# A four-mixer block on one core: second buffers for two delta-rule inputs, other priorities and planned latencies, and side work on TensorE gathered into visits

## The chip, the cores and the metric

The kernel runs on one core of one Trainium2 chip. Times are device microseconds (us). The kernel before took 2264.02 us as the median of three runs (2262.28 to 2264.04). Five engines work side by side: TensorE (PE, with its weight loads as PEld), VectorE (DVE), ScalarE (ACT), GpSimd (POOL) and SyncE (SP), which only issues DMAs here.

## The reference

The input x has 512 tokens of 2048 channels. A normalized x is multiplied by one large matrix w_in, and the columns of the product feed four sequence mixers with 1024 channels each, and a gate z of 4096. The mixers' outputs, times silu(z), go through w_out and are added to x:

```python
h = rms_norm(x, norm_g[l])
p = jnp.einsum('bsd,dn->bsn', h, w_in[l])
p_rwkv, p_fox, p_gdn, p_diff, z = jnp.split(p, bounds, axis=-1)
y = jnp.concatenate([rwkv7_time_mix(p_rwkv, ...), forgetting_attention(p_fox, ...),
                     gated_deltanet(p_gdn, ...), differential_attention(p_diff, ...)], axis=-1)
x = x + jnp.einsum('bsm,md->bsd', y * jax.nn.silu(z), w_out[l])
```

Two mixers are recurrences over time. RWKV-7 updates a 64x64 state per head at each token. The gated delta rule (GDN) does the like with q, k and v that come out of a causal convolution of four taps and a silu; the reference states it by chunks, with a triangular solve in each chunk. The other two are softmax attentions with a decay (FOX) and as a difference of two maps (DIFF). All is float32.

## The kernel before, in words

**Products.** Float32 products with w_in and w_out are made of three float32r products each: hh·wh, hl·wh and hh·wl, with h and l for the rounded part and the rest. A weight tile `wr` of 512 KB comes by DMA on SP's queue (three buffers, L318); ACT rounds it to `wh` (L313) and DVE subtracts to `wl` (L314), two buffers each. `gemm_fm` makes 128 output channels for all 512 tokens (three matmuls of 512 columns, then a yield), `gemm_tm` makes 256 channels with tokens on partitions (matmuls of 256 columns, a yield after six).

**Passes.** `main` loops over j = 0..7; each j is 128 channels of each mixer. A pass streams, in this order, the products for RWKV r, k, v; GDN v, k, q; FOX q and k; both attentions' v; DIFF q and k. After the last pass the z products follow, first for 16 tiles of y with smaller j (two of them run in pass 0), then the other 16, and then the product with w_out.

**Threads.** Beside the stream, generators do the mixers' own work in small steps: `rwkv_local`, `gdn` (with `gdn_local`, then `inverses`), `rwkv_chain` (8 chunks of 64 tokens, three steps each), `gdn_chain` (4 chunks of 128), `fox` and `diff`. `inverses` solves 32x32 blocks on DVE (L970, L971: 31 steps) and merges them on PE; only then do both chains of that j start. The next j's RWKV blocks wait for the chain before (`until("rwkv_half", j-1, q)` in `rwkv_local`), the next `inverses` waits for those blocks (`until("BK", j)`), and `gdn_local` begins with `until("gdn_chain", j-1)`.

**The order on PE is written by a planner** at the end of `hybrid_kernel`, when the kernel is built. It keeps a clock `pe[0]`, to which every matmul adds its estimated cost (L65 to L75). A thread that yields `w` comes due at `pe + 1.25*w` (`spawn`, SLACK 1.25). While the stream is not held up, the planner takes a due thread ahead of the next step of the stream, so threads can be visited after any step of 0.64 us on that clock. `free(bank)` and `until(event)` poll in the same way, at 1.25 and 0.6 us. The stream yields what it needs before its products may leave PSUM, as `("gdn_chain", j-1)` before GDN's k and q leave it (their SBUF tiles `gc_k`, `gc_q` have one buffer each). While that is not done, the planner takes threads alone and sets the clock forward to each one's due time; no stream product then stands between their matmuls.

PE executes that order strictly, waiting on semaphores. The other engines' orders come from the tile framework's own simulated schedule, with priorities: `band(PRIO_CHAIN)` before `PRIO_W` (weight loads and splits), `PRIO_EVAC`, `PRIO_MIX` and last `PRIO_FILL`. `put_y` writes a mixer's finished y to DRAM; it is read again when z is gated.

Of the kernel before, what the change touches and what calls it, by code (L numbers as in the profile page):

```python
# [20 lines left out]
P = 128  # L21
# [21 lines left out]

SLACK = 1.25

PRIO_CHAIN = 0
PRIO_W = 1_000_000
PRIO_EVAC = 2_000_000
# [6 lines left out]
def hybrid_kernel(ctx: ExitStack, tc: tile.TileContext, ins, out, steps=tuple(range(NJ)), ydbg=None, tail=True):  # L55
# [3 lines left out]
    STT = nc.vector.scalar_tensor_tensor  # L59
    ACT = nc.scalar.activation  # L60
    pe = [0.0]

    def MM(o, a, b, side=1, **kw):

        n, m = math.prod(b.shape[1:]), math.prod(a.shape[1:])  # L65
        if a.dtype == F32:
            pe[0] += 4 * max(n, m, 32) / 2400 / side
        else:
            pe[0] += max(n, 256 if a.dtype == F32R else 128) / 2400 / side
        return nc.tensor.matmul(o, a, b, **kw)  # L70

    def transpose(o, a):
        pe[0] += 0.108
        return nc.tensor.transpose(o, a, ident)

# [140 lines left out]
    for part in range(4):  # L216
        if part == 2:
            load_x(1)
        wr = wp.tile([P, 1024], F32, name=f"w0r{part}", tag="wr", bufs=3) if part < 2 else \
            mp.tile([P, 1024], F32, name=f"w0r{part}")  # L220
        load_tm(wr, part, FOX0 + 2 * G, DIFF0 + 2 * G)
        w0.append((wr, mp.tile([P, 1024], F32R, name=f"w0h{part}"), mp.tile([P, 1024], F32R, name=f"w0l{part}")))
# [92 lines left out]
        return wh, wl  # L315

    def wtile():
        return wp.tile([P, WN], F32, name=f"wr{wcount[0]}", tag="wr", bufs=3)  # L318

    def gemm_fm(c0, name, then=None):  # L320
        acc = None
# [44 lines left out]
    ydr = [dr.tile([P, T], F32, name=f"ydr{m}") for m in range(MT)]  # L366

    def put_y(m, y):
        nc.sync.dma_start(ydr[m], y)
        if ydbg is not None:  # L370
            nc.sync.dma_start(ydbg[m], y)

# [321 lines left out]
    def rwkv_chain(j, st, XT):  # L694
# [7 lines left out]
        for c in range(NCH):  # L702
            AR, ET, BKt, ZV = (st[n][c // 4][:, c % 4] for n in ("AR", "ET", "BKt", "ZV"))
            yield from free("cr")
            ps = bank("cr", f"pC{j}_{c}", 1.0e9)

            for h in range(2):
                hs = slice(h * C, (h + 1) * C)
                MM(ps[0:R_, P + h * C:P + (h + 1) * C], ET[:, h, 0:R_], ZV[:, hs], start=True, stop=True)
            if c:  # L710
                MM(ps[:, 0:P], AR.rearrange("p a t -> p (a t)"), Sb, start=True, stop=True)
            nc.scalar.copy(rs[0:C], ps[0:C, P:2 * P])
            yield 2.4
            y = yt[(c % 2) * C:(c % 2 + 1) * C, c // 2, :]
            if c:
                band(PRIO_CHAIN)
                TT(rs[0:C], rs[0:C], ps[0:C, 0:P], op=ALU.add)
                band(PRIO_MIX)
                nc.scalar.copy(y, ps[C:P, 0:P])
            for h in range(2):  # L720
                hs = slice(h * C, (h + 1) * C)
                MM(ps[0:R_, 2 * P + h * C:2 * P + (h + 1) * C], ET[:, h, 0:R_], rs[:, hs], start=True, stop=True)
            yield 2.0
            band(PRIO_CHAIN)
            nc.vector.tensor_copy(ZV[0:C, :], ps[0:C, 2 * P:3 * P])
            band(PRIO_MIX)
            for h in range(2):
                hs = slice(h * C, (h + 1) * C)
                MM(ps[C:P, 3 * P + h * C:3 * P + (h + 1) * C], ET[:, h, R_:R_ + C], ZV[:, hs], start=True, stop=True)

            if c < NCH - 1:
                for h in range(2):
                    hs = slice(h * C, (h + 1) * C)
                    MM(ps[hs, P:P + C], BKt[:, h], ZV[:, hs], side=2, start=True, stop=True)
            pe[0] += 0.2
            if c < NCH - 1:
                band(PRIO_CHAIN)
                W = Wc[:, c:c + 1]
                tS = mp.tile([P, C], F32, name=f"tS{j}_{c}", tag="tS", bufs=1)
                for h in range(2):  # L740
                    hs = slice(h * C, (h + 1) * C)
                    if c:
                        TS(tS[hs, :], Sb[hs, hs], W[hs, :], None, op0=ALU.mult)
                for h in range(2):
                    hs = slice(h * C, (h + 1) * C)
                    o = ps[hs, P:P + C]
                    if c:
                        STT(Sb[hs, hs], o, W[hs, :], tS[hs, :], op0=ALU.mult, op1=ALU.add)
                    else:
                        TS(Sb[hs, hs], o, W[hs, :], None, op0=ALU.mult)  # L750
                band(PRIO_MIX)
            if c:
                TT(y, y, ps[C:P, 3 * P:4 * P], op=ALU.add)
            else:
                nc.scalar.copy(y, ps[C:P, 3 * P:4 * P])
            release(f"pC{j}_{c}", 3.0)
            if c % 4 == 3:
                done.add(("rwkv_half", j, c // 4))

# [24 lines left out]
    def gdn_evac(j, i, acc):  # L784
        s = "qkv"[i]
        n = 8 * i + j
        if s == "v":
            a = mp.tile([P, T], F32, name=f"gc_{s}{j}", tag="gc_v", bufs=1)
        else:
            a = mp.tile([P, T], F32, name=f"gc_{s}{j}", tag=f"gc_{s}", bufs=1)  # L790
        ACT(a, acc, AF.Copy, scale=convw(3, n))
        for d in (1, 2, 3):
            STT(a[:, d:T], acc[:, 0:T - d], convw(3 - d, n), a[:, d:T], op0=ALU.mult, op1=ALU.add)
        return a
# [19 lines left out]
        return pt  # L814

    def gdn_local(j, res):

        yield from until("gdn_chain", j - 1)
        GA = mp.tile([P, NT, 2, P], F32, name=f"GA{j}", tag="GA", bufs=1)
        Dm = GA[:, :, 1, :]  # L820
        nc.gpsimd.dma_start(Dm, gcd[:, j, :].unsqueeze(0).to_broadcast([P, NT, P]))
        gdn_silu(j, "v", res["v"])
        yield 2.5
        band(PRIO_FILL)
        for c in range(NT):
            for b in range(4):
# [5 lines left out]
                                fill=0.0, base=0, channel_multiplier=-1)  # L832
        band(PRIO_MIX)

        yield from until("gk", j)
        k2 = res["k"]
        gdn_silu(j, "k", k2)
        yield 7.0
        yield from free("tr")
        pt = gdn_transposed(j, "k", k2)  # L840
        KTs = mp.tile([P, NT, P], F32, name=f"KTs{j}", tag="KTs", bufs=1)
# [15 lines left out]
        vn = mp.tile([P, NT, P], F32, name=f"vn{j}", tag="vn", bufs=1)  # L857
        TT(vn, pt.rearrange("p (t f) -> p t f", f=P), vn_s.unsqueeze(2).to_broadcast([P, NT, P]), op=ALU.mult)

        yield from until("gq", j)  # L860
        q2 = res["q"]
        gdn_silu(j, "q", q2)
        yield 8.0
        for q in range(2):
            yield from free("sc")
            ps = psc(f"pK{j}_{q}", 2.5)
# [16 lines left out]
    def gdn_chain(j, st, XG):  # L883
# [3 lines left out]
        for c in range(NT):  # L887
# [3 lines left out]
            if c:  # L891
                MM(ps[:, 0:P], k2[:, cs], S, start=True, stop=True)
                MM(ps[:, P:2 * P], q2[:, cs], S, start=True, stop=True)
                rs = mp.tile([P, P], F32, name=f"grs{j}_{c}", tag="gs", bufs=4)
                band(PRIO_CHAIN)
                STT(rs, ps[:, 0:P], eg_neg[:, c, j:j + 1], vn[:, c, :], op0=ALU.mult, op1=ALU.add)
                band(PRIO_MIX)
                ACT(ot[:, c, :], ps[:, P:2 * P], AF.Copy, scale=eg[:, 0, c, j:j + 1])
            else:
                rs = vn[:, 0, :]  # L900
            yield 2.4
            MM(ps[:, 2 * P:3 * P], XG[:, c, :], rs, start=True, stop=True)
            Y = mp.tile([P, P], F32, name=f"gY{j}_{c}", tag="gs", bufs=4)
            band(PRIO_CHAIN)
            nc.scalar.copy(Y, ps[:, 2 * P:3 * P])
            band(PRIO_MIX)
            yield 2.4
            if c < NT - 1:
                MM(ps[:, 0:P], KTs[:, c, :], Y, start=True, stop=True)
            MM(ps[:, 3 * P:4 * P], GA[:, c, 1, :], Y, start=True, stop=True)  # L910
# [8 lines left out]
            else:  # L919
                TS(ot[:, c, :], ps[:, 3 * P:4 * P], -1.0, None, op0=ALU.mult)  # L920
            band(PRIO_MIX)
            release(f"pG{j}_{c}", 3.2)
        done.add(("gdn_chain", j))
        sq = mp.tile([P, T], F32, name=f"osq{j}", tag="tmp", bufs=2)
        ACT(sq, ot.rearrange("p t f -> p (t f)"), AF.Square)
# [23 lines left out]
    def inverses(j, ET, GA, blk, start_rwkv):  # L949
# [14 lines left out]
        nc.gpsimd.memset(Xf[64:112, 1:512:34], 1.0)  # L964
        pr = lcp.tile([112, 512], F32, name=f"bP{j}", tag="lc", bufs=8)
        for t in range(1, 32):
            band(PRIO_FILL)
            n, w = (t + 1) // 2, t + 1
            pv_ = pr[:, 0:n * w].rearrange("p (a b) -> p a b", b=w)
            TT(pv_, X[:, 0:n, 0:w], A[:, 0:w, t].unsqueeze(1).to_broadcast([112, n, w]), op=ALU.mult)  # L970
# [20 lines left out]
        XQ = mp.tile([P, 4, 32], F32, name=f"XQ{j}", tag="gs", bufs=4)  # L991
        for g in range(4):
            nc.gpsimd.dma_start(XQ[32 * g:32 * g + 32], xb[16 + g:32:4].rearrange("m s t -> s m t"))
        yield 14.5
        yield from until("rwkv_local", j)

        XN = lcp.tile([P, 16, 32], F32, name=f"XN{j}", tag="lc", bufs=8)
# [84 lines left out]
    def qk_heads(j, ev, kind):  # L1082
# [1 line left out]
        gi = 0 if kind == "fox" else 2  # L1084
        TS(ss, ss, 1.0 / C, 1e-6, op0=ALU.mult, op1=ALU.add)
        rs = rsqrt(mp, ss, 16, "qk", f"{kind}{j}")
        yield 3.0
        rv = rs.rearrange("p (t s h) -> p t s h", t=NT, s=2)
        for s, dst in enumerate((qa, ka)):
            dv = dst.rearrange("p t (h f) -> p t h f", f=C)  # L1090
            TT(dv, dv, rv[:, :, s].unsqueeze(3).to_broadcast([P, NT, 2, C]), op=ALU.mult)
        yield 1.2

        parts = []
        for s, src in enumerate((qa, ka)):
# [189 lines left out]
    def main():  # L1285
# [15 lines left out]
        for j in steps:  # L1301
# [21 lines left out]
            for i in (2, 1, 0):  # L1323
                s_ = "qkv"[i]
                acc = yield from gemm_fm(GDN0 + i * G + j * P, f"g{s_}{j}")
                yield "gdn_chain" if i < 2 else "gdn_local", j - 1
                band(PRIO_EVAC)
                gres[s_] = gdn_evac(j, i, acc)
                done.add(("g" + s_, j))
                if i == 2:  # L1330
                    spawn(2.5, gdn(j, gres, local))
# [36 lines left out]
        v_evac(V0)(b, accs0[b])  # L1368

    stream, need = main(), None  # L1370
    with tc.manual_schedule(engines={nc.tensor.engine}):
        while stream is not None or threads:
            wait = stream is None or (need is not None and need not in done)
            if threads and (wait or threads[0][0] <= pe[0]):
                at_, _, gen = heapq.heappop(threads)
                pe[0] = max(pe[0], at_)
                band(PRIO_MIX)
                try:
                    spawn(next(gen), gen)
                except StopIteration:  # L1380
                    pass
            else:
                try:
                    need = next(stream)
                except StopIteration:
# [108 lines left out]
```

## Time and profile before

| | |
|---|---|
| median of 3 runs | 2264.02 us |
| the profiled execution | 2263.21 us, of which its span 2261.5 us |
| granted TensorE clock, mean over the span | 0.993 |
| busy: PE, PEld, DVE, ACT, POOL | 2209.2, 1893.5, 1363.8, 804.5, 246.7 us |
| chain that ended last, by engine | PE 90%, DVE 5%, POOL 2%, DMA 1%, ACT 1%, issue 1% |
| DMA | 226.33 MB, mean 100 GB/s |

Matmuls are pipelined: a row's duration (0.39 us for 512 columns) is longer than the distance to the next start, and the distances of starts tell the rate. "Idle before" is the engine's own wait ahead of an instruction, and behind the arrow stands what ended it. A pass is the time from one j's first `acc_r` product to the next j's.

### The profile page before, as it was taken

To read this page: it belongs to the slowest core of one execution; us is meant where nothing else is said; L and a number is where in the kernel's file an instruction comes from. 1 tells how busy PE (TensorE), PEld (TensorE's weight loads), DVE (VectorE), ACT (ScalarE), POOL (GpSimd) and SP (SyncE) were. 2 spreads that over 40 slices of the span, in tenths; PEclk is the share of its full clock that TensorE was granted. 3 is DMA by queue.
4 is the path that set the end of the run, shared out by engine and by line. 5 is a ranking of instruction groups with operands and counts; after the bars stand their busy time and mean duration, and the time that the engine had idled before them with its cause. 6 is when DMAs were issued, how large, how long until landed. Compare 5 with 4: busy or idle time off the path is not lost.

```text
span 2261.5 us, 37256 instructions
## 1 busy us (share of the span) xinstructions
PE 2209.2 (98%) x14604; PEld 1893.5 (84%) x14604; DVE 1363.8 (60%) x3601; ACT 804.5 (36%) x1504; POOL 246.7 (11%) x506
## 2 busy tenths in 40 slices
PE   7999999999999999999999999899999999999999
PEld 6789789879878977987997897798788888888887
DVE  6368588576857957767685695776553434322222
ACT  4233443443353343344335334334422223321121
POOL 2200121112102011110210211111000000100000
PEclk9999999999999999999999999999999999999999
DMA  5433323323322332332332333233346444654443
GB/s 167 104 88 94 97 74 90 97 66 94 98 72 73 93 96 58 94 101 61 85 107 63 80 82 98 65 96 105 96 137 181 119 125 120 163 136 116 113 125 75
DMA packets 321874, 226.33 MB, mean 100 GB/s; under 512 B 17423, under 2 KB 285394, under 8 KB 321186
## 3 DMA queue, kind: packets, MB, share of 16 engines
q1 hardware_dynamic: 298722, 187.05, 31.3%
q0 software_dynamic: 9152, 15.37, 3.2%
q10 hardware_dynamic: 13824, 21.54, 2.9%
q8 instruction: 115, 1.88, 0.3%
q14 instruction: 61, 0.50, 0.1%
HBM read 203.93 MB, written 19.97 MB: 99 GB/s over the span
## 4 chain that ended last, share of the span: by engine, by line
PE 90%; DVE 5%; POOL 2%; DMA 1%; ACT 1%; issue 1%; SPq 0%; ACTq 0%; DVEq 0%
PE acc_z L70 16%; PE acc_o L70 15%; PE acc_dqk L70 8%; PE acc_fqk L70 8%; PE acc_vv L70 6%; PE acc_k L70 4%; PE acc_v L70 4%; PE acc_r L70 4%; PE acc_gv L70 4%; PE acc_gk L70 4%; PE pC L70 3%; POOL GA L828 2%; PE acc_gq L70 2%; PE pG L70 1%; PE pSf L70 1%; DMA GA<-gcd 1%
## 5 line engine op out<-in xcount | busy, mean ns | idle before, releaser
L314 DVE TENSOR_TENSOR wl<-wr,wh 128x1024 fp32r<-128x1024 f32 x318 | 389.0, 1224 | 534.5 <-ACT wh L313 527.7
L313 ACT CAST wh<-wr 128x1024 fp32r<-128x1024 f32 x318 | 333.9, 1050 | 750.8 <-PE acc_o L70 231.8
L70 PE MATMUL acc_z<-hh,wh 128*128 128x512 f32 x512 | 204.5, 399 | 0.0
L70 PE MATMUL acc_z<-hh,wl 128*128 128x512 f32 x512 | 199.7, 390 | 0.0
L70 PE MATMUL acc_z<-hl,wh 128*128 128x512 f32 x512 | 199.6, 390 | 0.0
L70 PE MATMUL acc_o<-wh,gl 128*128 128x512 f32 x512 | 183.6, 389 | 0.0
L70 PE MATMUL acc_o<-wl,gh 128*128 128x512 f32 x512 | 177.6, 389 | 0.0
L70 PE MATMUL acc_o<-wh,gh 128*128 128x512 f32 x512 | 176.2, 389 | 0.0
L70 PE MATMUL acc_fqk<-wh,hh 128*128 128x256 f32 x512 | 151.8, 296 | 0.8 <-DVE gssk L807 0.8
L70 PE MATMUL acc_fqk<-wl,hh 128*128 128x256 f32 x512 | 145.1, 283 | 0.0
L70 PE MATMUL acc_fqk<-wh,hl 128*128 128x256 f32 x512 | 144.9, 283 | 0.0
L70 PE MATMUL acc_dqk<-wh,hh 128*128 128x256 f32 x512 | 138.2, 292 | 0.0
L970 DVE TENSOR_TENSOR bP<-bX,bA 112x2 f32<-112x2 f32 (+30 forms) x248 | 122.1, 492 | 24.1 <-POOL bA L958 18.5
L70 PE MATMUL acc_dqk<-wh,hl 128*128 128x256 f32 x512 | 133.6, 283 | 0.0
L70 PE MATMUL acc_vv<-wh,hh 128*128 128x256 f32 x448 | 120.4, 290 | 0.0
L70 PE MATMUL acc_vv<-wh,hl 128*128 128x256 f32 x448 | 116.9, 282 | 0.0
L70 PEld LDWEIGHTS acc_z<-hh,wl 128*128 128x128 f32 x512 | 96.1, 188 | 20.5
L70 PEld LDWEIGHTS acc_o<-wl,gh 128*128 128x128 f32 x512 | 96.1, 188 | 20.2 <-DVE wl L314 0.3
L70 PEld LDWEIGHTS acc_o<-wh,gl 128*128 128x128 f32 x512 | 96.1, 188 | 20.0
L70 PEld LDWEIGHTS acc_o<-wh,gh 128*128 128x128 f32 x512 | 96.0, 188 | 20.1 <-ACT wh L313 0.2
L70 PEld LDWEIGHTS acc_z<-hh,wh 128*128 128x128 f32 x512 | 96.2, 188 | 19.4 <-issue 0.7
L70 PEld LDWEIGHTS acc_z<-hl,wh 128*128 128x128 f32 x512 | 96.3, 188 | 18.4
(515 smaller groups left out, 5226.4 us busy)
## 6 DMA issues: line engine op xcount, KB each, us to landing
wr<-in_w_in SPq DMA_DIRECT2D x162, 512.0 KB
wr<-in_w_in SPq DMA_DIRECT2D x184, 256.0 KB
wr<-in_w_out SPq DMA_DIRECT2D x64, 512.0 KB
zy<-ydr ACTq DMA_DIRECT2D x30, 256.0 KB
nb<-cdr SPq DMA_DIRECT2D x8, 512.0 KB
xo<-in_x ACTq DMA_DIRECT2D x16, 256.0 KB
gr<-gdr POOLq DMA_DIRECT2D x16, 256.0 KB, 5.1
out<-xo ACTq DMA_DIRECT2D x16, 256.0 KB
```

The source lines that it names most:

```text
L70: return nc.tensor.matmul(o, a, b, **kw)
L313: nc.scalar.copy(wh[:, 0:n], wr[:, 0:n])
L314: TT(wl[:, 0:n], wr[:, 0:n], wh[:, 0:n].bitcast(F32), op=ALU.subtract)
L828: nc.gpsimd.tensor_scalar(Dm[:, c, bs], Dm[:, c, bs], gcx[:, b, c * 8 + j:c * 8 + j + 1], 0.0, op0=ALU.subtract, op1=ALU.min)
L970: TT(pv_, X[:, 0:n, 0:w], A[:, 0:w, t].unsqueeze(1).to_broadcast([112, n, w]), op=ALU.mult)
```

## The change: what it does

1. **Buffers.** `gc_k` and `gc_q` get two buffers, `wr` two in place of three. The stream's k and q now need only the chain of j-2. `gdn_local` does all three silus first, each as soon as its product is there, and only then waits for the chain of j-1.
2. **Bands and queues.** The copy of y in the RWKV chain (L719) and the scaling of `ot` in the GDN chain (L898) move from MIX to CHAIN. The solve's 31 steps move from FILL to MIX. `put_y` issues on POOL's queue in place of SP's.
3. **Planned latencies.** Shorter in both chains and ahead of the merge of the inverses, longer in `qk_heads`.
4. **Visits.** A thread may be taken only when the stream has run at least STRETCH = 1.5 us of the planner's clock since its last return from threads that issued matmuls, or while such a visit lasts (`away`), or when the stream is held up.

```diff
-        wr = wp.tile([P, 1024], F32, name=f"w0r{part}", tag="wr", bufs=3) if part < 2 else \
+        wr = wp.tile([P, 1024], F32, name=f"w0r{part}", tag="wr", bufs=2) if part < 2 else \
...
-        return wp.tile([P, WN], F32, name=f"wr{wcount[0]}", tag="wr", bufs=3)
+        return wp.tile([P, WN], F32, name=f"wr{wcount[0]}", tag="wr", bufs=2)
...
-        nc.sync.dma_start(ydr[m], y)
+        nc.gpsimd.dma_start(ydr[m], y)
...
-            yield 2.4
+            yield 1.8
             y = yt[(c % 2) * C:(c % 2 + 1) * C, c // 2, :]
             if c:
                 band(PRIO_CHAIN)
                 TT(rs[0:C], rs[0:C], ps[0:C, 0:P], op=ALU.add)
+                nc.scalar.copy(y, ps[C:P, 0:P])
                 band(PRIO_MIX)
-                nc.scalar.copy(y, ps[C:P, 0:P])
...
-            yield 2.0
+            yield 1.5
...
-            release(f"pC{j}_{c}", 3.0)
+            release(f"pC{j}_{c}", 2.4)
...
-            a = mp.tile([P, T], F32, name=f"gc_{s}{j}", tag=f"gc_{s}", bufs=1)
+            a = mp.tile([P, T], F32, name=f"gc_{s}{j}", tag=f"gc_{s}", bufs=2)
...
     def gdn_local(j, res):
+        gdn_silu(j, "v", res["v"])
+        yield 2.5
+        yield from until("gk", j)
+        k2 = res["k"]
+        gdn_silu(j, "k", k2)
+        yield 2.5
+        yield from until("gq", j)
+        q2 = res["q"]
+        gdn_silu(j, "q", q2)
+        yield 2.5
 
         yield from until("gdn_chain", j - 1)
...
-        gdn_silu(j, "v", res["v"])
-        yield 2.5
...
-        yield from until("gk", j)
-        k2 = res["k"]
-        gdn_silu(j, "k", k2)
-        yield 7.0
...
-        yield from until("gq", j)
-        q2 = res["q"]
-        gdn_silu(j, "q", q2)
-        yield 8.0
+        yield 4.0
...
+                ACT(ot[:, c, :], ps[:, P:2 * P], AF.Copy, scale=eg[:, 0, c, j:j + 1])
                 band(PRIO_MIX)
-                ACT(ot[:, c, :], ps[:, P:2 * P], AF.Copy, scale=eg[:, 0, c, j:j + 1])
...
-            yield 2.4
+            yield 2.0
             MM(ps[:, 2 * P:3 * P], XG[:, c, :], rs, start=True, stop=True)
...
-            yield 2.4
+            yield 1.8
...
-            release(f"pG{j}_{c}", 3.2)
+            release(f"pG{j}_{c}", 2.6)
...
-            band(PRIO_FILL)
+            band(PRIO_MIX)
             n, w = (t + 1) // 2, t + 1
...
-        yield 14.5
+        yield 12.5
         yield from until("rwkv_local", j)
...
-        yield 3.0
+        yield 4.0
         rv = rs.rearrange("p (t s h) -> p t s h", t=NT, s=2)
...
-        yield 1.2
+        yield 2.0
...
-                yield "gdn_chain" if i < 2 else "gdn_local", j - 1
+                yield ("gdn_chain", max(j - 2, steps[0] - 1)) if i < 2 else ("gdn_local", j - 1)
...
+    away, since = False, 0.0
...
-            if threads and (wait or threads[0][0] <= pe[0]):
+            ready = threads and threads[0][0] <= pe[0] and (away or pe[0] - since >= STRETCH)
+            if threads and (wait or ready):
                 at_, _, gen = heapq.heappop(threads)
                 pe[0] = max(pe[0], at_)
                 band(PRIO_MIX)
+                n = issued[0]
                 try:
                     spawn(next(gen), gen)
                 except StopIteration:
                     pass
+                away = away or issued[0] > n
             else:
+                if away:
+                    away, since = False, pe[0]
```

`issued` counts the calls of MM and transpose.

## Rows read from the trace of the kernel before

**Rows 1.** The page: engines' busy us (share of the span), and costly groups.

```profile
PE 2209.2 (98%) x14604; PEld 1893.5 (84%) x14604; DVE 1363.8 (60%) x3601; ACT 804.5 (36%) x1504; POOL 246.7 (11%) x506
...
L970 DVE TENSOR_TENSOR bP<-bX,bA 112x2 f32<-112x2 f32 (+30 forms) x248 | 122.1, 492 | 24.1 <-POOL bA L958 18.5
```

**Rows 2.** Waits of PE: instruction <- what ended it, us in total, times, longest us.

```profile
PE pC L70 <- ACT yt L719: 20.0, 7, 3.4
...
PE ptfox L74 <- DVE qafox L1091: 6.1, 6, 1.1
```

**Rows 3.** Passes 2, 3 and 4 by engine; behind the busy times PEclk, DMA, GB/s.

```profile
413.00:598.00 185.00, 181.18 (x1402) 158.91 (x1401) 133.47 (x402) 74.21 (x156) 26.45 (x55) 1.00 0.31 82
598.00:788.00 190.00, 185.48 (x1417) 161.90 (x1416) 135.81 (x404) 76.38 (x160) 27.79 (x57) 0.98 0.32 84
788.00:978.00 190.00, 184.55 (x1418) 161.37 (x1417) 135.63 (x405) 76.30 (x160) 26.79 (x57) 0.99 0.32 84
```

**Rows 4.** Timeline of PE, 680 to 693 us: start, duration, instruction, count, wait.

```profile
680.48 1.16 PE L70 MATMUL pA<-AR,BK 64*128 64x128 f32 x16
681.57 0.45 PE L70 MATMUL pC<-ZV,ET 128*66 128x64 f32 x4
...
686.39 0.71 PE L70 MATMUL pC<-rs,ET 128*66 128x64 f32 x4 [3.44 <-ACT yt L719]
...
687.30 0.77 PE L70 MATMUL acc_gq<-hh,wh 128*128 128x512 f32 x1
...
692.62 0.27 PE L70 MATMUL pC<-ZV,ET 128*64 128x64 f32 x1
```

**Rows 5.** Busy times by engine just after that wait.

```profile
688.00:692.00 4.00, 4.00 (x11) 3.13 (x10) 3.70 (x22) 1.78 (x3) 0.72 (x1) 0.50 0.52 60
```

**Rows 6.** Timeline of PE: the first and the last short run between two visits.

```profile
244.06 0.60 PE L74 MATMUL pPf<-ident,prf 128*128 128x128 f32 x4
...
245.99 0.45 PE L70 MATMUL pmr<-XN,ET 32*32 32x32 f32 x32
...
1661.71 0.39 PE L70 MATMUL acc_z<-hh,wl 128*128 128x512 f32 x1
1661.94 0.60 PE L74 MATMUL pgo<-ident,vn 128*128 128x128 f32 x4
1662.29 0.48 PE L70 MATMUL acc_z<-hh,wh 128*128 128x512 f32 x1
1662.61 0.40 PE L70 MATMUL acc_z<-hl,wh 128*128 128x512 f32 x1
...
1663.86 0.27 PE L70 MATMUL pC<-ZV,ET 128*64 128x64 f32 x1
```

**Rows 7.** Timeline of PE: one turn from RWKV chain to RWKV chain.

```profile
631.46 0.40 PE L70 MATMUL pC<-ZV,ET 128*66 128x64 f32 x4
...
731.37 0.45 PE L70 MATMUL pC<-ZV,ET 128*64 128x64 f32 x4
...
740.71 0.60 PE L74 MATMUL pB<-ident,BK 128*128 128x128 f32 x4
...
814.73 0.45 PE L70 MATMUL pmr<-XN,ET 32*32 32x32 f32 x32
...
821.62 0.40 PE L70 MATMUL pC<-ZV,ET 128*66 128x64 f32 x4
```

**Rows 8.** Timelines of DVE and PE: a chain step's sum, and the matmul on it.

```profile
658.96 0.27 DVE L717 TENSOR_TENSOR rs<-rs,pC 64x128 f32<-64x128 f32 x1
...
661.68 0.40 PE L70 MATMUL pC<-rs,ET 128*66 128x64 f32 x4
```

**Rows 9.** Weight splits while z streams (DVE, ACT), and a DMA of the page.

```profile
1702.90 1.23 DVE L314 TENSOR_TENSOR wl<-wr,wh 128x1024 fp32r<-128x1024 f32 x1 [4.06 <-ACT wh L313]
...
1712.74 1.05 ACT L313 CAST wh<-wr 128x1024 fp32r<-128x1024 f32 x1 [4.38 <-PE acc_z L70]
...
gr<-gdr POOLq DMA_DIRECT2D x16, 256.0 KB, 5.1
```

More of the change, by code (lines that the diff above doesn't have):

```diff
@@ L44 @@
 SLACK = 1.25
+STRETCH = 1.5
 PRIO_CHAIN = 0
@@ L61, in hybrid_kernel @@
     pe = [0.0]
+    issued = [0]
     def MM(o, a, b, side=1, **kw):
+        issued[0] += 1
         n, m = math.prod(b.shape[1:]), math.prod(a.shape[1:])
@@ L72, in transpose @@
     def transpose(o, a):
+        issued[0] += 1
         pe[0] += 0.108
```

## The prediction

> **What bounds the kernel now.** I read the page first, then PE's waits, the passes, and PE's order row by row. The page gives TensorE 98% of the span and POOL 11% [rows 1]: no other engine is near, so time can only go where PE waits, runs at the lower clock, or spends more than its products need. Each has its view.
>
> *Waits.* One place holds most of the wait: seven times a matmul of the RWKV chain waits, 20.0 us in all, and six times the FOX transposes, 6.1 us [rows 2]. The timeline shows where the first kind sits [rows 4]: between GDN's k and q products. There the stream needs `("gdn_chain", j-1)`, so the planner lines up thread work alone: pA, pC, pB, then the pC that waits 3.44 us. Nothing streams in between, so PE reaches a chain step before ACT and DVE have done theirs.
>
> *Clock.* Right behind that wait the granted clock is 0.50 (1.2 GHz) for the whole of 688 to 692 us, against 1.00 (2.4 GHz) in an undisturbed pass [rows 3, 5]. Twelve q products take 5.32 us there [rows 4]; at the 0.23 us from one start to the next that full clock shows [rows 6], they take 2.76.
>
> *Passes.* Pass 2 (413 to 598) takes 185 us at 1.00; pass 3 takes 190 at 0.98, pass 4 190 at 0.99, and three more like it follow [rows 3]. The difference is that wait and its clock.
>
> *Changes between stream and threads.* Take the visit of four transposes at 1661.94 [rows 6]. From the last z product's start before it to the second one's after it is 0.90 us. Two stream steps take 0.46, four transposes at the pace of sixteen pA (1.09/16 = 0.068 us each, [rows 4]) 0.27. The visit itself costs 0.17; half of it is the first product after it, 0.32 to the next start in place of 0.23. From 230 us on there are 461 visits, some 58 a pass, and 174 of them follow a run of only one or two steps of the stream (first and last in [rows 6]).
>
> **The change part by part**, against the profiled execution (2263.2 us: span 2261.5 and 1.7 around it; the median shown, 2264.0, is 0.8 above).
>
> 1. *Second buffers of k and q; need of j-2.* The hold between k and q is gone. The same thread matmuls must still run, now with stream products between them, so only waits and clock are gained: -20.0 us; clock 2.6 in pass 3 and up to 1% of 190 = 1.9 us in each of four passes, together -10. Upper end -30; lower end 0, if the same step is late elsewhere. I take -30, and charge new lateness in 5.
>
> 2. *qk_heads 3.0 to 4.0 and 1.2 to 2.0.* The last of these waits, about 1 us each [rows 2], is met by 0.8 x 1.25 = 1.0 us more lead, and the first yield gives another 1.25. -6 (0 to -6.1).
>
> 3. *Visits.* On the planner's clock a step is 0.64 us, so 1.5 us means three steps: the 174 visits after shorter runs move to the next allowed point and mostly join another. Each joined visit saves at most 0.17; a change from thread to thread may cost something of its own, though sixteen pA pass into pC without a gap [rows 4]. I take 0.13: 174 x 0.13 = -22.6. Bounds: 0 if visits only shift, and 231 x 0.17 = -39 if half of the 461 go.
> The Trainium skill ("TensorE: Matmul & The Clock Gate", Part 2, step 1) says that PE pulls the next weight load ahead of running matmuls, so the next tile's weights load meanwhile; by that rule a return would cost nothing and this part would give 0, 2238 in all. The 0.32 against 0.23 us speaks against it.
>
> 4. *What threads lose by waiting for a visit.* The loop that could set the pace is RWKV's [rows 7]: chain from 631.46 to 731.37 (99.9 us), blocks to 740.71 (9.3), solve to 814.73 (74.0), merge to the next chain's start at 821.62 (6.9): 190 us, as long as the pass. Eight chunks lose (0.6 + 0.5 + 0.6) x 1.25 = 2.1 us each, 17 in all; the merge is due 2.5 us sooner. The stretch rule adds to some 40 resumptions in that loop (24 of the chain, 7 of the solve, the rest polls and blocks) between 0 and 1.3 us each; with 2 in 5 visits held back I take 0.35: +14. The loop comes out near 190 - 19.5 + 14 = 184, less some 3 us because visits get cheaper: 181. PE's own work in a pass is 190 - 3.4 - 1.05 - 1.9 - 58 x 0.38 x 0.13 (2.9) = 181. Both meet; neither adds.
>
> 5. *Shorter chain latencies.* PE waits in order, so a late sum stops the stream behind it. In the crowded stretch rs is ready at 659.23 and its matmul starts at 661.68 [rows 8]: 2.45 us of lead, of which the change takes 0.75. So most steps stay covered. Priority of L719 and L898 helps a little. I charge 1.3 us a pass, +10 in all; ends: 0, and 0.4 us on each of 288 chain steps, +115 (a rival).
>
> 6. *The solve from FILL to MIX.* 122.1 us of products over 248 instructions [rows 1], and their sums, no longer give way to softmax work emitted later. 0; up to +20 if FOX's transposes wait for it, down to -5 where the merge had waited.
>
> 7. *Two `wr` buffers.* A third tile in flight goes; the load of tile n+2 now starts when tile n is split. In the z stretch this is 1704.13, and the cast of n+2 starts at 1712.74, 8.6 us later, waiting for PE, not for DMA [rows 9]. A 256 KB transfer lands 5.1 us after its issue there; doubling all of that would be 10, and behind the cast a tile's 24 products give PE 24 x 0.23 = 5.5 us, of which cast and subtraction take 1.05 + 1.23. So 0; +10 at most, in the columns of w_out where x and the output move too.
>
> 8. *put_y on POOL, silus first, GA later.* 32 issues leave SP, where a late y held back weights behind it, and stand in POOL's order instead; y is not read before z is gated. POOL is 11% busy [rows 1]. 0, -3 to +5. GA's DMA and POOL work now starts with the wait for the chain, beside the k transposes; `inverses` waits for the RWKV blocks anyway, 0.
>
> Sum: -30 - 6 - 22.6 + 10 = -48.6; 2263.2 - 48.6 = 2214.6, and with the 0.8 of the median **2215 us**. By passes: five from about 190 to 182 (-40), two from 185 to 182 (-5), 3 in the stretch of z with threads: the same.
>
> **The rivals.**
> - *The thread loop sets the pace.* If held visits cost 0.5 us a resumption more than I took, the loop is 187 to 189, the stream runs ahead until it needs `rwkv_local` or, at the end, `inverses`. It gains about 2 us in five passes and 3 behind: 2250 (2236 to 2262). For it: the loop equals the pass today [rows 7]. Against: the hold slows the loop itself, 3.44 us of wait in one chunk.
> - *Chain steps come late.* This ends on the other side. DVE, 71% busy in a pass (135.81 of 190, [rows 3]), executes in a fixed order; with 0.6 to 0.75 us less lead, and solve steps ahead of softmax, PE meets unfinished sums. 288 chain steps: the gain of 59 us is gone at 0.2 us a step; at 0.35 it is +100, **2305**, the lower clock behind longer waits included. For it: the 3.44 us are of this kind. Against: 2.45 us of lead in a full stretch.
> - *Changes cost nothing, or visits do not get fewer*: 2215 + 22.6 = 2238.
> - *Half the visits go, and nothing new waits*: 2263 - 30 - 6 - 39 = 2188, 2189 as a median.
>
> **How the numbers follow.** Chances: forecast 0.48 (own range 2200 to 2232), loop 0.20, late chain 0.17, no gain from visits 0.06, half the visits 0.09. About 0.2% (4.5 us) is what a measurement can tell from no change. Slower: 0.16 out of the late chain. Within: 0.01 of it and 0.04 of the loop's top. Faster: the rest, 0.79. For the range I leave out the late chain's 0.16 at the top and 0.04 below 2180: 2180 to 2264.
>
> **What would show it.** Right: no wait of pC on L719 near 3.4 us and clock 1.00 in all passes; ptfox waits gone; some 290 visits from the second pass on in place of 461; no stream run under three steps except beside a hold; passes of 181 to 183 us. The loop rival shows as passes of 187 or more, or as threads alone on PE ahead of RWKV's r or of the z tiles; the late chain as many waits of pC, pG or pPf on DVE and ACT. It is wrong if PE waits for `wl` or `wh`, or if there are fewer visits and the time per visit grows as much.

## The result, and the profile after

| | before | after |
|---|---|---|
| median of the runs of this comparison | 2263.15 us (2261.82 to 2264.04) | **2236.96 us** (2235.21 to 2238.55) |
| span of the profiled execution | 2261.5 us | 2233.4 us |
| mean granted TensorE clock | 0.993 | 0.997 |

The ratio is 0.9885, with a 95% interval of 0.9867 to 0.9902: 26 us faster, where 49 were forecast. The time lies inside the range, but outside the forecast's own 2200 to 2232.

The page after, busy time of the engines, and the solve's line that [rows 1] showed (busy, mean ns | idle before it):

```profile
span 2233.4 us, 37352 instructions
...
PE 2197.7 (98%) x14604; PEld 1890.0 (85%) x14604; DVE 1377.5 (62%) x3601; ACT 799.5 (36%) x1504; POOL 260.1 (12%) x538
...
L977 DVE TENSOR_TENSOR bP<-bX,bA 112x2 f32<-112x2 f32 (+30 forms) x248 | 122.1, 492 | 9.4 <-POOL bA L965 4.4
```

The same number of matmuls keeps PE busy for 11.5 us less. PE's waits after (us in total, times, longest), to be read against [rows 2]:

```profile
PE pC L75 <- ACT yt L724: 12.1, 14, 2.5
...
PE pC L75 <- DVE ZV L731: 1.7, 3, 0.6
...
PE acc_o L75 <- ACT wh L319: 0.7, 1, 0.7
```

The 3.4 us waits and all six of ptfox are gone. But the profile still shows the RWKV chain waiting on the copy of y, 14 times and shorter: 12.1 us where there were 20.0. Passes 2, 3 and 4 after, in the columns of [rows 3]:

```profile
413.00:599.00 186.00, 184.06 (x1434) 161.39 (x1432) 137.70 (x404) 77.39 (x161) 28.79 (x61) 1.00 0.32 88
599.00:782.00 183.00, 181.07 (x1407) 159.78 (x1404) 137.22 (x403) 74.36 (x159) 29.17 (x61) 1.00 0.32 86
782.00:968.00 186.00, 184.04 (x1433) 161.23 (x1432) 138.70 (x405) 77.45 (x163) 28.81 (x61) 1.00 0.32 86
```

The clock is 1.00 in these passes, and in those behind them; pass 1 has one fall of it, behind a wait of 2.5 us (323 to 327 us: 0.57). From pass 2 on they take 182 to 186 us, on average 184.3 (before 189.2) and not 181 to 183. So the waits and the clock came back about as forecast, and the rest has to be looked for inside PE's busy time. From the starts of all PE rows between the start of pass 2 (413 us) and the first z product (six passes) I split the time into five parts. The stream alone, 806.3 us, is the same in every kernel. "Border" is what PE needs above that rate when it enters a visit and at the first product after it; "inside" is from the first start of a visit to the first start of the stream behind it, less the waits, and the change of thread is part of it:

| us in six passes | before | after | after, no stretch rule | before, stretch rule only | before, buffers only | last two runs: rule and short latencies / neither |
|---|---|---|---|---|---|---|
| PE waits | 30.3 | 11.4 | 13.3 | 33.6 | 7.7 | 17.7 / 4.4 |
| lower clock and rest | 11.3 | 4.1 | 4.9 | 10.1 | 4.3 | 5.5 / 4.4 |
| border | 45.8 | 36.1 | 43.7 | 37.2 | 43.3 | 36.7 / 43.8 |
| inside visits | 241.1 | 247.5 | 238.8 | 255.0 | 237.5 | 245.1 / 236.8 |
| visits | 352 | 300 | 360 | 282 | 370 | 300 / 365 |
| sum with the stream | 1135 | 1106 | 1107 | 1142 | 1099 | 1111 / 1096 |

From before to after: waits -18.9, clock and rest -7.2, border -9.7, inside +6.4; together -29.4. What is new is in the row "inside visits": two thirds of what the border saves come back there.

One gathered visit after the change, PE's timeline (start, duration, instruction, count):

```profile
663.00 0.39 PE L75 MATMUL acc_gk<-hh,wl 128*128 128x512 f32 x1
663.23 0.95 PE L75 MATMUL pn<-bonesr,rw_k 128*128 128x2 f32 x8
664.04 0.47 PE L75 MATMUL pd<-V,prd 128*128 128x128 f32 x2
664.44 0.44 PE L75 MATMUL pSd<-Khdiff,Qhdiff 64*128 64x384 f32 x2
...
665.16 0.45 PE L75 MATMUL pC<-ZV,ET 128*66 128x64 f32 x4
665.45 0.44 PE L75 MATMUL pC<-Sb,AR 128*128 128x128 f32 x2
665.72 0.39 PE L75 MATMUL pG<-Sg,gc_k 128*128 128x128 f32 x2
665.95 0.39 PE L75 MATMUL pG<-Sg,gc_q 128*128 128x128 f32 x2
666.09 0.48 PE L75 MATMUL acc_gk<-hh,wh 128*128 128x512 f32 x1
666.41 0.39 PE L75 MATMUL acc_gk<-hl,wh 128*128 128x512 f32 x1
```

Four threads share one way back, at the old price: 0.32 us from 666.09 to the next start. Before the stream, the two gc_q products take 0.14 us (665.95 to 666.09). In the kernel before, the same two stand ahead of another thread's products and take 0.33 (timeline of PE, before):

```profile
678.73 0.49 PE L70 MATMUL pG<-Sg,gc_k 128*128 128x128 f32 x2
679.06 0.39 PE L70 MATMUL pG<-Sg,gc_q 128*128 128x128 f32 x2
679.39 1.16 PE L70 MATMUL pd<-V,prd 128*128 128x128 f32 x8
```

So it is with three of four kinds of group in the kernel before (median from first start to the next start behind the group): pG's four matmuls 0.36 us between stream and stream (5 cases) and 0.66 between threads (7), six pSd 0.55 (8) and 0.91 (6), six pC 0.43 (27) and 0.56 (13). Eight pC are free of it, 0.49 in both places.

### The profile page after: what moved, and what is told of

It reads as the page before. It is cut to its first block, busy times and chain, and to the rows that moved or that the text cites. A ratio compares the mean times of both kernels' runs of the same rounds, so it can differ in the third digit from the quotient of the medians.

```text
span 2233.4 us, 37352 instructions
## 1 busy us (share of the span) xinstructions
PE 2197.7 (98%) x14604; PEld 1890.0 (85%) x14604; DVE 1377.5 (62%) x3601; ACT 799.5 (36%) x1504; POOL 260.1 (12%) x538
## 4 chain that ended last, share of the span: by engine, by line
PE 90%; DVE 3%; DMA 3%; POOL 3%; ACT 2%; issue 1%; SPq 0%; ACTq 0%; DVEq 0%; POOLq 0%
PE acc_z L75 16%; PE acc_o L75 15%; PE acc_dqk L75 8%; PE acc_vv L75 8%; PE acc_fqk L75 7%; PE acc_v L75 4%; PE acc_k L75 4%; PE acc_r L75 4%; PE acc_gv L75 3%; PE acc_gk L75 3%; PE pC L75 3%; POOL GA L842 2%; PE acc_gq L75 2%; DMA GA<-gcd 2%; PE pG L75 1%; PE pSf L75 1%
```

## The experiments

The medians of before beside these runs are 2262.91 to 2263.49 us; each ratio is to the runs of before on the same chip.

**The stretch rule taken out** of the changed kernel.

```diff
-STRETCH = 1.5
+STRETCH = 0.0
```

> The changed kernel with STRETCH = 0.0: threads are taken as soon as they are due, as before the change; all else as changed. The order on PE then has 496 visits in place of 420. Theory A (joined visits save little, about 0.08 us each, since a change from thread to thread costs nearly as much as one from and to the stream): about +6 us, 2243 (2240 to 2247), waits of the chains as they were or a few us more. Theory B (a visit costs the 0.17 us that I read off one of them): +13 us, 2250 or more. Theory C (gathering costs more in late chain steps than it saves): faster than 2237.

Measured: 2238.0 us, ratio 0.9893 (0.9878 to 0.9908): 1 us from the changed kernel, which the intervals can't tell from nothing, and none of the three theories. The table's columns two and three show why: 60 visits fewer save 7.6 us at the border and cost 8.7 inside.

**The stretch rule alone**, put into the kernel before (its lines of the change and `issued`, nothing else).

```diff
+STRETCH = 1.5
...
+            ready = threads and threads[0][0] <= pe[0] and (away or pe[0] - since >= STRETCH)
+            if threads and (wait or ready):
```

> The kernel before with the stretch rule alone: 399 visits in place of 490, one buffer for k and q, old bands, old latencies, three weight buffers. Theory A (0.08 us a visit): -7 us, about 2256, the waits of 3.4 us between k and q still there. Theory B (0.17 us): -15 us, about 2248. Theory C (held visits lengthen the chain loop, which then sets the pace): longer holds ahead of q, 2263 or slower.

Measured: 2277.69 us, ratio 1.0067 (1.0054 to 1.0079): slower, as in theory C. Waits of PE and passes 3 to 5, in the columns of [rows 2, 3]:

```profile
PE pC L74 <- ACT yt L724: 18.6, 14, 3.6
```

```profile
605.00:797.00 192.00, 185.47 (x1419) 162.81 (x1418) 137.01 (x405) 76.35 (x161) 27.43 (x57) 0.98 0.30 80
797.00:988.00 191.00, 186.02 (x1414) 162.35 (x1413) 139.48 (x405) 75.44 (x158) 27.05 (x57) 0.98 0.32 85
988.00:1176.00 188.00, 182.91 (x1420) 160.76 (x1419) 134.38 (x402) 76.10 (x160) 27.38 (x57) 1.00 0.31 83
```

By the table the border is 8.6 us less than before, but PE's waits are 3.3 more and the inside 13.9. The passes fit a loop of the recurrences that is longer because every resumption waits for a visit, with the holds still in the stream; how much of the 13.9 is threads that run alone, and how much changes between threads, this run doesn't part.

**The buffers alone**: part 1 of the change in the kernel before.

```diff
-            a = mp.tile([P, T], F32, name=f"gc_{s}{j}", tag=f"gc_{s}", bufs=1)
+            a = mp.tile([P, T], F32, name=f"gc_{s}{j}", tag=f"gc_{s}", bufs=2)
...
-                yield "gdn_chain" if i < 2 else "gdn_local", j - 1
+                yield ("gdn_chain", max(j - 2, steps[0] - 1)) if i < 2 else ("gdn_local", j - 1)
```

(with the silus ahead of the wait and two `wr`)

> The kernel before with the second buffers of gc_k and gc_q, two weight buffers, the need of j-2 and the three silus first in gdn_local; nothing else of the change. Theory A (the removed hold is nearly all of the gain): the waits of 3.4 us and the half clock behind them go, passes of 184 to 185 us, 2240 (2235 to 2247); the FOX transposes still wait 1 us a pass. Rival (the hold only moves, because the chain loop of 190 us sets the pace): passes stay at 188 to 190, about 2258.

Measured: 2239.75 us, ratio 0.9898 (0.9884 to 0.9911). This is 23.5 of the 26 us. The copy of y, 20.0 us before, is down to this (PE's waits):

```profile
PE pC L70 <- ACT yt L719: 0.6, 2, 0.4
```

Its six passes are even 6 us shorter than those of the changed kernel. It gives that back at the end: from the first z product on it takes 722 us, the changed kernel 715. There PE waits 4.1 us in place of 0.7, and the clock is at 0.50 for 6.8 us from 1562 us on. The last pass's threads reach 160 us into z in place of 143, but that this is the reason isn't shown: in the run with short latencies in the last pass, below, they reach 140, and the stretch still takes 719.

**The latencies of before** in the changed kernel: 2.4, 2.0 and 3.0 in the RWKV chain, 2.4, 2.4 and 3.2 in GDN's, 14.5 before the merge.

```diff
-            yield 1.8
+            yield 2.4
             y = yt[(c % 2) * C:(c % 2 + 1) * C, c // 2, :]
...
-        yield 12.5
+        yield 14.5
```

> The changed kernel with the planned latencies of before in both chains and ahead of the merge (2.4, 2.0, 3.0; 2.4, 2.4, 3.2; 14.5). Theory A (the chain loop has room, PE's own work sets the pass): the 12 us of waits on L724 go, passes near 183, about 2227. Rival (the loop sets the pace as soon as it is longer): the loop grows by up to 8 x 2.1 + 2.5 = 19 us, the stream is held ahead of RWKV's r or of the z tiles, 2245 to 2290.

Measured: 2300.04 us, ratio 1.0167 (1.0153 to 1.0181): 63 us slower than the changed kernel, and 10 beyond the rival's range. Passes 3 and 4, the last stretch of the passes, and as long a stretch behind the first z product (1538), in the columns of [rows 3]:

```profile
591.00:766.00 175.00, 173.29 (x1332) 152.52 (x1330) 120.56 (x332) 71.64 (x150) 20.75 (x42) 1.00 0.33 87
766.00:960.00 194.00, 189.34 (x1430) 165.75 (x1431) 140.08 (x409) 76.38 (x164) 29.88 (x61) 0.97 0.30 82
...
1385.00:1537.00 152.00, 151.60 (x1196) 136.91 (x1194) 106.84 (x301) 60.20 (x125) 21.53 (x43) 1.00 0.31 81
1538.00:1690.00 152.00, 130.05 (x795) 102.90 (x795) 96.17 (x279) 47.23 (x107) 17.17 (x33) 0.87 0.31 87
```

The stream first runs ahead of the threads, 175 us for a pass; then it reaches what it needs and goes at their pace, 192 to 194. The last solve and chain are left over when the passes are done: 22 us of waits behind 1538, at a clock of 0.87. The loop sets the pace here, and the shorter latencies are what pays for the stretch rule.

**Old chain latencies without the stretch rule** (12.5 kept).

```diff
-STRETCH = 1.5
+STRETCH = 0.0
...
-            yield 1.8
+            yield 2.4
             y = yt[(c % 2) * C:(c % 2 + 1) * C, c // 2, :]
```

> The changed kernel without the stretch rule (STRETCH = 0.0) and with the chain latencies of before (2.4, 2.0, 3.0 and 2.4, 2.4, 3.2); the 12.5 ahead of the merge and all else stay as changed. Theory A (the shorter latencies only repair what the stretch rule does to the chain loop, and cost some 10 us of waits on L724): those waits go, passes near 182 us as in the kernel with the buffers alone, 2230 (2226 to 2234). Rival (without the shorter latencies the loop is too long at the end, and the z tiles are held for the last inverses): 2238 to 2242.

Measured: 2236.91 us, ratio 0.988 (0.9864 to 0.9896), with 7.1 us of waits on the copy of y (7, the longest 2.7): between theory A and the rival. Rule and short latencies taken out together leave the time where it is.

**The solve back in FILL.**

```diff
-            band(PRIO_MIX)
+            band(PRIO_FILL)
             n, w = (t + 1) // 2, t + 1
```

> The changed kernel with the solve's 31 steps back in FILL. Theory A (the solve has slack on either side): 2237, within 3 us. Rival (with the merge due 2.5 us sooner the solve is late in FILL, and PE waits in the merge for XN or ET): 5 to 20 us slower.

Measured: 2237.77 us, ratio 0.9888 (0.9873 to 0.9904): no effect.

**The yields of `qk_heads` back** (3.0 and 1.2).

```diff
-        yield 4.0
+        yield 3.0
         rv = rs.rearrange("p (t s h) -> p t s h", t=NT, s=2)
```

> The changed kernel with the yields of before in qk_heads (3.0 and 1.2). Theory A (step 2 of the prediction): about 1 us of wait before the FOX transposes in each pass comes back, 2243 (2240 to 2245). Rival (held visits give that lead anyway): 2237, no waits there.

Measured: 2238.74 us, ratio 0.989 (0.9876 to 0.9904). No wait of ptfox even so, but six of pPd on DVE's BKt that the changed kernel doesn't have (4.7 us, the longest 0.8). What gives the FOX transposes their lead, the spacing of the visits or the new order, isn't shown. The long yields buy at most 2 us, which the intervals can't tell from nothing.

**Two `wr` alone**, in the kernel before.

```diff
-        return wp.tile([P, WN], F32, name=f"wr{wcount[0]}", tag="wr", bufs=3)
+        return wp.tile([P, WN], F32, name=f"wr{wcount[0]}", tag="wr", bufs=2)
```

> The kernel before with two weight buffers in place of three, nothing else. Theory A (the third buffer hides nothing): 2263, within 2 us, no waits of PE on wl or wh beyond 2 us. Rival (weights come late in the z and w_out stretches): 2268 to 2290, waits of acc_z and acc_o on wh or wl.

Measured: 2264.18 us, ratio 1.0006 (0.9997 to 1.0014). Its one new wait is acc_o on wh, 1.4 us.

**Buffers alone, with short RWKV latencies in the last pass only**, 12.5 before the merge and the new `qk_heads` yields.

```diff
-            yield 2.4
+            yield 1.8 if j == steps[-1] else 2.4
             y = yt[(c % 2) * C:(c % 2 + 1) * C, c // 2, :]
```

> The kernel with the buffers alone (second buffers, need of j-2, silus first), and with three parts of the change beside it: the RWKV chain's shorter latencies in the last pass only, 12.5 ahead of the merge, and the yields of qk_heads as changed. Theory A (that kernel's passes of 182 us are PE's own work, and it loses 7 us behind them because the last inverses hold the z tiles): z begins near 1515 us and takes 713 to 716 to the end, 2230 (2226 to 2234), faster than the changed kernel by 3 to 11 us. Rival (what the passes gain is given back behind them in any order): 2236 to 2240.

Measured: 2239.38 us, ratio 0.9896 (0.988 to 0.9913): no gain over the buffers alone. 7.5 us of waits on the copy of y came with it, and z began at 1518 us in place of 1516.

**The copies of y and ot back in MIX**, on the kernel without rule and with old chain latencies.

```diff
                 band(PRIO_CHAIN)
                 TT(rs[0:C], rs[0:C], ps[0:C, 0:P], op=ALU.add)
-                nc.scalar.copy(y, ps[C:P, 0:P])
                 band(PRIO_MIX)
+                nc.scalar.copy(y, ps[C:P, 0:P])
```

> The kernel without the stretch rule and with the old chain latencies, with the copies of y (L724) and of ot (L904) back in MIX. Theory A (the waits on L724 there, 7.1 us, come from the step's sum on DVE being late, which the copy's band does not change): 2237, waits within 3 us of the same. Rival (the copy in CHAIN is what delays the step, since the kernel with the buffers alone has no such waits): the waits go, 2230.

Measured: 2237.05 us, ratio 0.9883 (0.9868 to 0.9898), waits on the copy 6.9 us. The band neither causes nor cures them. Theory A has the time right but not its reason: in the trace of the kernel that this run starts from, only 1.2 of the 7.1 us have passed when the sum on DVE ends; the rest is the copy's.

**The copy of y behind the matmuls on rs**, in the changed kernel. The matmul on rs waits for the copy although it needs only the sum; both touch the PSUM tile pC.

```diff
                 TT(rs[0:C], rs[0:C], ps[0:C, 0:P], op=ALU.add)
-                nc.scalar.copy(y, ps[C:P, 0:P])
                 band(PRIO_MIX)
             for h in range(2):
                 hs = slice(h * C, (h + 1) * C)
                 MM(ps[0:R_, 2 * P + h * C:2 * P + (h + 1) * C], ET[:, h, 0:R_], rs[:, hs], start=True, stop=True)
+            if c:
+                band(PRIO_CHAIN)
+                nc.scalar.copy(y, ps[C:P, 0:P])
+                band(PRIO_MIX)
```

> The changed kernel with the copy of y in the RWKV chain (L724) issued behind the two matmuls on rs instead of ahead of them, so that they no longer wait for it. Theory A (the 12.1 us of waits are the copy's own lateness, behind a weight cast in ACT's fixed order, while the sum on DVE is done): the waits go, 2226 (2223 to 2230), faster than both kernels. Rival (the sum is late and the copy only lands last): as many us of waits on the sum instead, 2237.

Measured: 2241.66 us, ratio 0.9905 (0.989 to 0.992): a miss, and if anything slower than the changed kernel. PE's waits, and one of them with what ran on ACT and DVE ahead of it (timelines in one order of time):

```profile
PE pC L75 <- DVE ZV L734: 13.9, 15, 1.6
...
PE pC L75 <- DVE rs L723: 5.9, 4, 2.1
```

```profile
521.52 0.63 ACT L808 ACTIVATE gt_q<-gc_q 128x512 f32<-128x512 f32 x1 [1.85 <-DVE rsq_do L166]
522.06 0.57 ACT L855 COPY KTs<-pgk 128x512 f32<-128x512 f32 x1
522.53 0.60 ACT L814 ACTIVATE gsqk<-pgk 128x512 f32<-128x512 f32 x1
523.15 0.26 ACT L730 COPY yt<-pC 64x128 f32<-64x128 f32 x1
523.39 0.68 DVE L815 TENSOR_REDUCE gssk<-gsqk 128x4 f32<-128x512 f32 x1
523.99 0.27 DVE L734 COPY ZV<-pC 64x128 f32<-64x128 f32 x1
524.32 0.27 PE L75 MATMUL pC<-ZV,ET 128*64 128x64 f32 x1 [1.63 <-DVE ZV L734]
```

The wait moved one step down the chain. The copy of y still stands behind three long ACT instructions, DVE's order now puts the copy of ZV behind it and behind a sum that uses their result, and the next matmul waits for ZV. Six of the 15 waits are like this one (9.2 us). In the other nine (4.7 us) the copy of y has been done for 0.5 us or more, and ZV stands behind a step of GDN's convolution on DVE (L802). The 5.9 us on rs are the rival's: there the sum itself is late.

**The same move on the kernel without rule and with old chain latencies.** The edit is the one above.

> The kernel without the stretch rule and with the old chain latencies, with the same copy issued behind the matmuls on rs. Theory A: its 7.1 us of waits on L724 go, 2230 (2227 to 2233); if the stretch rule is worth nothing, it ends within 4 us of e11_copy_after. Rival: 2237, waits on the sum.

Measured: **2230.44 us** (2227.24 to 2231.45), ratio 0.9856 (0.9839 to 0.9872): 6 to 7 us below the same kernel without the move and below the changed kernel, the fastest of all; this interval overlaps theirs by 0.0008 and 0.0005. It lies in theory A's range, but 11 us from the run above, where at most 4 were expected if the rule is worth nothing. PE's waits, and DVE's on the copy of y:

```profile
PE pC L75 <- DVE ZV L734: 1.4, 3, 0.7
PE pC L75 <- DVE rs L723: 1.0, 2, 0.6
```

```profile
DVE ZV L734 <- ACT yt L730: 15.9, 14, 3.4
```

Here DVE waits for the copy too, but hardly any of it reaches PE; the chain's planned lead behind that matmul is 2.0 x 1.25 = 2.5 us here, against 1.9 in the run above. That this is the reason isn't shown.

## Why the prediction was right or wrong

**Step 1, the holds: right.** It said -20.0 of waits and -10 of clock. With the buffers alone the copy of y went from 20.0 to 0.6 us, six passes lost 22.6 us of waits and 7.0 of clock and rest, and 23.5 us of the median went. In the changed kernel it is -18.9 and -7.2 with all else that PE waits for.

**Step 2, the FOX transposes: right in size, wrong in cause.** All 6.1 us went, but with the old yields as well (2238.74 us, though with 4.7 us of waits elsewhere). With the buffers alone two waits of 3.2 us in all were left.

**Step 3, the visits: this step failed.** The forecast was 174 x 0.13 = -22.6. With the rule against without it, all else as changed, 60 visits fewer save 7.6 us at the border and cost 8.7 inside, so +1.1. In the last two runs, which differ in the latencies too, 65 fewer save 7.1 and cost 8.3. Gathering gave nothing of the 22.6, and that is the whole distance of 22 to the forecast. The -9.7 and +6.4 from before to after are not its worth alone, for the buffers change the order too: by themselves they have -2.5 and -3.6, with 18 visits more.

Each of its terms was off. The number: no run of the stream is now under three of its steps, but, to go by how many went, most of the 174 held visits don't meet one that waits already. They move later and push the next ones; there are 70 fewer from 230 us on (461 to 391). The price of a border is 7.6/60 = 0.13 or 7.1/65 = 0.11 us, where 0.17 was read off one visit; in the table's split 0.09 of that visit is border (0.32 in place of 0.23) and the rest the time of its four transposes. And the price of a change from thread to thread, taken as 0.04 beside the one pair pA and pC that shows none, is 8.7/60 = 0.14 or 8.3/65 = 0.13. The two prices cancel. The prediction's last sentence named this: fewer visits, and the time per visit grows as much.

Its rival "changes cost nothing, or visits do not get fewer" gave 2238, one us from the time, but not by its reasons: visits did get fewer, and changes do cost. Behind "changes cost nothing" stood the rule in "TensorE: Matmul & The Clock Gate" (Part 2, step 1) of the Trainium skill, that the next tile's weights load while the present one streams. By it a return would be free; the trace still has 0.32 us against 0.23 at 666.09.

**Step 4, the loop: the balance was right.** A pass is 184.3 us, of it 182.4 without PE's waits, and the chain's turn is as long (starts at 630, 815, 999, 1184); both were forecast at 181. That the two stand so close is shown from the other side: with the rule and without the shorter latencies passes are 188 to 192 in one run and 192 to 194 in the other. The rival "the loop sets the pace" came in both.

**Step 5, late sums: right in size (12.1 us on y against 10), right in cause for less than half.** It priced rs, the sum that the matmul needs. The profile names the copy of y, which lands last. In nine of the 14 waits, 5.4 us, the sum is done and the copy alone is late, in ACT's queue behind the rounding of a weight tile, as here (ACT, DVE and PE after, in one order of time):

```profile
668.19 0.26 DVE L723 TENSOR_TENSOR rs<-rs,pC 64x128 f32<-64x128 f32 x1
668.50 1.03 ACT L319 CAST wh<-wr 128x1024 fp32r<-128x1024 f32 x1
669.56 0.26 ACT L724 COPY yt<-pC 64x128 f32<-64x128 f32 x1
669.87 0.45 PE L75 MATMUL pC<-rs,ET 128*66 128x64 f32 x4 [1.24 <-ACT yt L724]
```

rs is ready at 668.45, the copy starts 1.1 us later behind the cast. The other five, 6.7 us, have another origin (POOL, ACT, DVE and PE after):

```profile
880.73 5.39 POOL L842 TENSOR_SCALAR GA<-GA,gcx 128x32 f32<-128x32 f32 x11
886.16 0.63 ACT L844 ACTIVATE GA<-GA 128x512 f32<-128x512 f32 x1 [3.79 <-POOL GA L842]
886.69 0.24 ACT L718 COPY rs<-pC 64x128 f32<-64x128 f32 x1
886.97 0.28 DVE L723 TENSOR_TENSOR rs<-rs,pC 64x128 f32<-64x128 f32 x1 [2.36 <-ACT rs L718]
887.28 0.26 ACT L724 COPY yt<-pC 64x128 f32<-64x128 f32 x1 [0.35 <-DVE rs L723]
887.60 0.45 PE L75 MATMUL pC<-rs,ET 128*66 128x64 f32 x4 [1.40 <-ACT yt L724]
```

ACT sits 3.79 us in front of GA's exponential until POOL has made its sums; both copies of the chain step queue behind it, and PE stands. The first of them feeds the sum, so the sum is late too: it ends at 887.25, 1.05 us after PE fell idle. Counted so over all 14, the sum accounts for 5.0 of the 12.1 us and the copy behind it for 7.1; the 5.9 us of waits on rs in the run with the copy moved fit that.

In the kernel before, the five long waits were the sum's for the most part: the copy there waited for the sum and came 0.3 us behind it (DVE and ACT, before):

```profile
685.77 0.27 DVE L717 TENSOR_TENSOR rs<-rs,pC 64x128 f32<-64x128 f32 x1
686.08 0.26 ACT L719 COPY yt<-pC 64x128 f32<-64x128 f32 x1 [3.25 <-DVE rs L717]
```

Of the 20.0 us before, the sum accounts for 15.4. The two short waits, 2.9 us, were the copy's alone, behind GA; ACT waited 30.6 us for POOL there in all. That GA is the cause of these is read from the traces; no run took it away.

**Steps 6 and 7: zero, as forecast**, each shown by a run of its own. **Step 8:** 32 issues more on POOL (busy 246.7 to 260.1 us) show no wait of z or of the output; no run has them alone. But "GA later: 0" looked only at who needs GA (`inverses`) and not at who queues behind it on ACT; by the row above it has a part in the 6.7 us.

**The chance of slower (a late chain, 0.16)** didn't come, but the slow side was near: the changed kernel with the latencies of before takes 2300 us, by the loop and not by late sums.

What stays open: why the ZV copy is late for PE in one of the last two runs and not in the other, which differ in the rule and in the chain's latencies, and no run parts the two; and why a change between two threads costs PE what it does.

## What to carry to other kernels

Before pricing a gathering of small work, count the borders that it makes as well as those it removes: here a visit's border with the stream cost 0.11 to 0.13 us and a change between two threads 0.13 to 0.14, so fewer visits saved nothing where 22 us were forecast. Count also the joins by replaying the order, not by the number of visits held back. In a kernel whose recurrent loop is as long as its stream, change latencies and gating together, and read an engine's queue ahead of a late instruction: here a copy of 0.26 us held PE up because of what stood before it. Where a profile names the last releaser, look also when the others landed.

## What the runs showed of the hardware

In the kernel before, a group of small float32 matmuls mostly took PE longer among other threads' groups than between stream products: six pSd 0.91 against 0.55 us, four pG 0.66 against 0.36; eight pC cost the same 0.49. Which pairs are free isn't settled. Two weight tiles in flight, of up to 512 KB, were as good here as three at 100 GB/s over the span (1.0006).
